# Down projections of 16 of 22 FFN tiles by seven block products instead of eight, and retention's prompt matmuls in another order

## The chip, the cores and the metric

The kernel runs on one core of a Trainium2 chip. The metric is the device time of one execution in microseconds. Before the change it is 1979.84 us, the median of three runs (1979.19 to 1980.41).

A core has a matrix engine (PE in the rows; its weight loads are listed apart as PEld), a vector engine (DVE), a scalar engine (ACT), GpSimd (POOL) and SyncE (SP), which issues most transfers. Each works through its own instructions in order. Matmuls write to PSUM, a small memory of banks that the vector and scalar engines read; everything else lies in SBUF.

## The reference, cut to what matters

One step of a two-layer decoder trunk on 512 prompt tokens and 8 sample tokens, in float32, width 1024. Each layer is

```
x += 0.5 * FFN1(rmsnorm(x))
z  = rmsnorm(x) @ w_in          # retention, windowed attention, conformer conv
x += concat(o_retention, o_attention, o_conv) @ w_out
x += 0.5 * FFN2(rmsnorm(x))
FFN(h) = (silu(h @ wg) * (h @ wu)) @ wd     # wg, wu: 1024 x 2816, wd: 2816 x 1024
```

Retention runs over chunks of 128 tokens with four heads: `o = (q k^T * decay) v + q S * decay`, where `S` is the state that the earlier chunks left.

## The kernel before, in words

Activations lie transposed: features on the 128 partitions, all 520 tokens along the row, so that x is 8 tiles of 128x520. A matmul covers one half of the tokens, 260. Full float32 accuracy comes from splitting each operand into a high part (rounded to the matrix engine's fast float32 format) and a low remainder, and adding three products: high weight with low data, high with high, low with high. This is `mm3` (L206 to L212): six matmuls of 128x260 for one 128x128 weight tile, three products on each half of the tokens.

Weights come in chunks of eight 128x128 tiles, 512 KB each, in the order of use. For each chunk SyncE loads it (`ensure_load`, L170), ACT rounds it to the high part (`split_hi`, L185, 128x1024) and DVE subtracts for the low part (`split_lo`, L192). Three chunks of each are buffered; `next_tile` starts the splits of the chunk two ahead whenever it enters a new one.

An FFN has 22 tiles of 128 hidden features, done in two groups of 11 (`NG`, `GF`). For each tile f the kernel computes gate and up (16 weight tiles, 96 matmuls), then DVE scales the gate (L288), ACT applies silu (L290), DVE scales the up part (L291) and multiplies (L292), and the product is split into high and low (L222 on ACT, L223 on DVE). When the 11 tiles of a group are there, the down projection loops over the 8 output tiles m; for each it adds 11 `mm3` products in PSUM, f from 0 to 10, and DVE adds half of the sum to x (L299). There are two layers with two FFNs each, so four FFNs.

PSUM is handed out in tiles of two banks, four of them in rotation (`ptile`). The program fixes the order on each engine by the order of the code (`manual_schedule`); between the FFNs the middle part (`mix`) follows a list of step names, `ORDER`. A wait on another engine is a semaphore and holds back everything behind it on the waiting engine.

In `mix`, `ret_prompt` computes retention for two chunks at a time (steps `ri2` and `ri0`). Its second half (L792 to L807) goes through the chunks and heads; for each it issues one matmul over all 128 partitions (L801, values times scores) and, for every chunk but the first, one over 64 partitions (L806, state times q; head 0 of a pair uses partitions 0 to 63, head 1 those from 64). These are plain float32 matmuls, and each leaves two records in the trace.

Of the kernel before, what the change touches and what calls it, by code (L numbers as in the profile page):

```python
# [10 lines left out]
F32 = mybir.dt.float32  # L11
# [11 lines left out]
NG = 2  # L23
GF = NF // NG
# [3 lines left out]
CT = 8  # L28
LNEXP, SILU = "natural_log_exp_and_others", "silu_and_others"
# [83 lines left out]

@with_exitstack
def step_kernel(ctx: ExitStack, tc: tile.TileContext, io: dict):
# [6 lines left out]
    wraw = pool("wraw", 3)  # L122
# [11 lines left out]
    R = const.tile([128, NT], F32, name="R")  # L134
    Rd = const.tile([128, 2, NT], F32, name="Rd")
# [33 lines left out]
    raw, spl, at, nxt, pending = {}, {}, [0], [0], []  # L169

    def ensure_load(i):
        if i < NCH and i not in raw:
            t = wraw.tile([128, CT * 128], F32, tag="w", name="w")
            nc.sync.dma_start(t, io["w"][i])
            raw[i] = t

    def split_hi(i):

        if i == nxt[0] and i < NCH:
            nxt[0] += 1  # L180
            ensure_load(i)
            t, raw[i] = raw[i], None
            h = wspl.tile([128, CT * 128], F32R, tag="wh", name="wh")
            lo = wspl.tile([128, CT * 128], F32R, tag="wl", name="wl")
            nc.scalar.copy(h, t)  # L185
            spl[i] = (h, lo)
            pending.append((i, t))

    def split_lo(n=9):
        for i, t in pending[:n]:  # L190
            h, lo = spl[i]
            nc.vector.tensor_sub(lo, t, h.bitcast(F32))  # L192
            ensure_load(i + 3)
        del pending[:n]

    def next_tile(ahead=True):
        i, c = divmod(at[0], CT)
        if c == 0 and ahead:
            for j in (i, i + 1, i + 2):
                split_hi(j)  # L200
            split_lo()
        at[0] += 1
        s = slice(c * 128, (c + 1) * 128)
        return spl[i][0][:, s], spl[i][1][:, s]
# [71 lines left out]

    def ffn(norm, after):
        for g in range(NG):
            hs = []
            for f in range(GF):  # L280
                first = g == 0 and f == 0
                og, ou = ptile(), ptile()
                for o, k in ffn_tiles(first, og, ou):
                    mm3(o, next_tile(), xh[:, k], xl[:, k], k == 0, k == KD - 1)
                if first:
                    run(norm)
                t, u = wt("t"), wt("u")
                nc.vector.tensor_mul(v2(t), og[:, :, :HN], v2(R))  # L288
                table(SILU)
                nc.scalar.activation(t, t, AF.Silu)  # L290
                nc.vector.tensor_mul(v2(u), ou[:, :, :HN], v2(R))  # L291
                nc.vector.tensor_mul(u, u, t)  # L292
                hs.append(v2(unit(F32R)))
                split(hs[f][:, 0], hs[f][:, 1], u)
            for m in range(KD):
                o = ptile()
                for f in range(GF):
                    mm3(o, next_tile(), hs[f][:, 0], hs[f][:, 1], f == 0, f == GF - 1)
# [3 lines left out]
                if g == NG - 1:  # L302
                    run(after(m))

    def mix(l, after):
# [467 lines left out]
        def ret_prompt(c0):  # L773
# [20 lines left out]
            oo = o.rearrange("p e (i a t) -> p e i a t", i=2, a=2)  # L794
            for i in range(2):
                c = c0 + i
                t = slice(c * 128, (c + 1) * 128)
                for h in range(4):
                    a, e = divmod(h, 2)
                    d, s = oo[:, e, i, a], slice(64 * e, 64 * e + 64)  # L800
# [84 lines left out]
        def chunk_hi():  # L885
            while True:
                split_hi(nxt[0])
# [31 lines left out]
    raw[0], raw[1] = (wraw.tile([128, CT * 128], F32, tag="w", name="w") for _ in range(2))  # L919
    spl[0], spl[1] = (  # L920
        tuple(wspl.tile([128, CT * 128], F32R, tag=t, name=t) for t in ("wh", "wl")) for _ in range(2)
    )
    nxt[0] = 2

# [22 lines left out]
    ensure_load(2)  # L947
    nc.sync.dma_start(cc, io["cc"])
    ensure_load(3)
    onef = const.tile([128, 128], F32, name="onef")  # L950
# [14 lines left out]
    for step in START:  # L965
        if step[0] == "h":
            half(half_split, int(step[1]))
        elif step[0] == "c":
            split_hi(int(step[1]))
# [23 lines left out]
def host_arrays(i):  # L993
# [16 lines left out]
    gu = [t.reshape(DEPTH, NG, -1, 128, 1024) for t in gu]  # L1010
    dn = [
        f[f"ffn{j}_wd"].reshape(DEPTH, NG, GF, 128, KD, 128).transpose(0, 1, 4, 2, 3, 5)
        .reshape(DEPTH, NG, GF * KD // CT, CT, 128, 128).transpose(0, 1, 2, 4, 3, 5)
        .reshape(DEPTH, NG, -1, 128, 1024)
        for j in (1, 2)
    ]
    ffn = [np.concatenate([g, d], axis=2).reshape(DEPTH, -1, 128, 1024) for g, d in zip(gu, dn)]
# [83 lines left out]
```

## Time and profile before

| | |
|---|---|
| median of three runs | 1979.84 us |
| the profiled execution, whole time | 1980.78 us |
| its span from first to last instruction | 1979.0 us |
| PE busy | 1955.9 us (99%), 16190 records |
| DVE busy | 984.2 us (50%) |
| ACT busy | 666.2 us (34%) |
| mean granted TensorE clock | 0.996 of full speed |

The profiled execution is 0.94 us above the median. Matmuls overlap in the engine's pipeline: one of 128x260 lasts 283 ns in its record, and the next starts 120 ns after it. What counts for the time is the distance from start to start; what counts for an engine that waits for a result is the end.

### The profile page before, as it was taken

To read this page: it belongs to the slowest core of one execution; us is meant where nothing else is said; L and a number is where in the kernel's file an instruction comes from. 1 tells how busy PE (TensorE), PEld (TensorE's weight loads), DVE (VectorE), ACT (ScalarE), POOL (GpSimd) and SP (SyncE) were. 2 spreads that over 40 slices of the span, in tenths; PEclk is the share of its full clock that TensorE was granted. 3 is DMA by queue.
4 is the path that set the end of the run, shared out by engine and by line. 5 is a ranking of instruction groups with operands and counts; after the bars stand their busy time and mean duration, and the time that the engine had idled before them with its cause. 6 is when DMAs were issued, how large, how long until landed. Compare 5 with 4: busy or idle time off the path is not lost.

```text
span 1979.0 us, 36417 instructions
## 1 busy us (share of the span) xinstructions
PE 1955.9 (99%) x16190; PEld 1936.6 (98%) x16190; DVE 984.2 (50%) x1311; ACT 666.2 (34%) x960; POOL 21.4 (1%) x48
## 2 busy tenths in 40 slices
PE   8999999999989999999999999999998999999999
PEld 8999999999889999999999999999997999999999
DVE  6443444488566443344444434445886564423442
ACT  5221223333665222222332212224337542212221
POOL 0000000000000000000000000000000000000000
PEclk9999999999999999999999999999999999999999
DMA  5222222333302222222222222223232122222231
GB/s 186 96 96 87 95 86 97 112 104 111 112 33 90 95 93 96 86 89 95 95 92 91 96 86 89 96 94 123 97 119 90 44 97 92 94 94 96 86 103 69
DMA packets 53581, 188.26 MB, mean 95 GB/s; under 512 B 6208, under 2 KB 6960, under 8 KB 53296
## 3 DMA queue, kind: packets, MB, share of 16 engines
q1 hardware_dynamic: 50784, 178.40, 26.6%
q0 software_dynamic: 2496, 7.43, 1.2%
q8 instruction: 127, 2.08, 0.4%
q14 instruction: 30, 0.25, 0.0%
q10 hardware_dynamic: 144, 0.11, 0.0%
HBM read 178.45 MB, written 7.45 MB: 94 GB/s over the span
## 4 chain that ended last, share of the span: by engine, by line
PE 97%; DVE 1%; ACT 1%; DMA 0%; issue 0%; SPq 0%; DVEq 0%
PE o L209 93%; PE o L228 1%; PE o L801 1%; PE o L806 0%; PE o L823 0%; DMA x<-in_x 0%; PE o L333 0%; PE o L594 0%; PE o L582 0%; DVE nt L246 0%; PE o L782 0%; DVE rr L247 0%; ACT rsq L836 0%; ACT m L567 0%; DVE m L859 0%
## 5 line engine op out<-in xcount | busy, mean ns | idle before, releaser
L209 PE MATMUL o<-xl,wh 128*128 128x260 f32 x3584 | 724.6, 283 | 7.2 <-DVE xl L254 5.9
L209 PE MATMUL o<-xh,wl 128*128 128x260 f32 x3584 | 723.0, 283 | 0.0
L209 PE MATMUL o<-xh,wh 128*128 128x260 f32 x3584 | 722.3, 283 | 0.0
L192 DVE TENSOR_TENSOR wl<-w,wh 128x1024 fp32r<-128x1024 f32 x318 | 389.0, 1224 | 424.7 <-ACT wh L185 422.7
L209 PEld LDWEIGHTS o<-xl,wh 128*128 128x128 f32 x3584 | 554.0, 189 | 8.4 <-ACT wh L222 5.8
L209 PEld LDWEIGHTS o<-xh,wl 128*128 128x128 f32 x3584 | 553.6, 189 | 0.0
L209 PEld LDWEIGHTS o<-xh,wh 128*128 128x128 f32 x3584 | 552.4, 189 | 0.0
L185 ACT CAST wh<-w 128x1024 fp32r<-128x1024 f32 x318 | 333.3, 1049 | 615.3 <-PE o L209 331.7
L209 PE MATMUL o<-m,wh 128*128 128x260 f32 x3072 | 493.0, 282 | 0.0
L209 PEld LDWEIGHTS o<-m,wh 128*128 128x128 f32 x3072 | 421.0, 188 | 0.0
L209 PE MATMUL o<-m,wl 128*128 128x260 f32 x1536 | 308.6, 282 | 0.0
L209 PEld LDWEIGHTS o<-m,wl 128*128 128x128 f32 x1536 | 236.5, 188 | 0.0
L291 DVE TENSOR_TENSOR u<-o,R 128x520 f32<-128x520 f32 x88 | 61.6, 699 | 248.6 <-PE o L209 248.6
L222 ACT CAST m<-u 128x520 fp32r<-128x520 f32 x88 | 55.2, 627 | 324.6 <-DVE u L292 324.6
L290 ACT ACTIVATE t<-t 128x520 f32<-128x520 f32 x88 | 56.2, 638 | 164.4 <-DVE t L288 164.4
L299 DVE SCALAR_TENSOR_TENSOR x<-o,x 128x520 f32<-128x520 f32 x64 | 44.7, 698 | 97.9 <-PE o L209 97.6
L223 DVE TENSOR_TENSOR m<-u,m 128x520 fp32r<-128x520 f32 x88 | 61.7, 701 | 61.1 <-ACT m L222 61.1
L411 DVE SCALAR_TENSOR_TENSOR m<-m,par 128x512 f32<-128x512 f32 x120 | 90.0, 750 | 2.9
L252 ACT ACTIVATE xh<-x,par 128x520 fp32r<-128x520 f32 x48 | 34.9, 729 | 99.3 <-DVE x L299 80.2
L292 DVE TENSOR_TENSOR u<-u,t 128x520 f32<-128x520 f32 x88 | 61.7, 701 | 9.2
L288 DVE TENSOR_TENSOR t<-o,R 128x520 f32<-128x520 f32 x88 | 60.9, 693 | 0.1
L254 DVE SCALAR_TENSOR_TENSOR xl<-x,par,xh 128x520 fp32r<-128x520 f32 x48 | 36.3, 758 | 21.5 <-ACT xh L252 21.5
(166 smaller groups left out, 664.8 us busy)
## 6 DMA issues: line engine op xcount, KB each, us to landing
w<-in_w SPq DMA_DIRECT2D x318, 512.0 KB, 3.2
out_y<-x SPq DMA_DIRECT2D x8, 260.0 KB, 2.3
m<-in_s_ret SPq DMA_DIRECT2D x4, 512.0 KB, 5.5
m<-sc POOLq DMA_DIRECT2D x8, 256.0 KB, 4.4
out_o_rets<-m POOLq DMA_DIRECT2D x4, 512.0 KB, 3.2
x<-in_x SPq DMA_DIRECT2D x3, 520.0 KB, 7.8
cc<-in_cc SPq DMA_DIRECT2D x1, 1092.0 KB, 10.4
w<-in_w SPq DMA_DIRECT2D x4, 256.0 KB, 6.4
```

Source lines behind the costliest of these rows:

```text
L185: nc.scalar.copy(h, t)
L192: nc.vector.tensor_sub(lo, t, h.bitcast(F32))
L209: nc.tensor.matmul(o[:, s, :HN], lhsT=a, rhs=b[:, s * HN : (s + 1) * HN], start=first and i == 0, stop=last and i == 2,)
L222: nc.scalar.copy(h, src)
L223: nc.vector.tensor_sub(lo, src, h.bitcast(F32))
L254: nc.vector.scalar_tensor_tensor(xl[:, k], x[:, k], g, xh[:, k].bitcast(F32), op0=ALU.mult, op1=ALU.subtract)
L288: nc.vector.tensor_mul(v2(t), og[:, :, :HN], v2(R))
L290: nc.scalar.activation(t, t, AF.Silu)
L291: nc.vector.tensor_mul(v2(u), ou[:, :, :HN], v2(R))
L292: nc.vector.tensor_mul(u, u, t)
L299: nc.vector.scalar_tensor_tensor(v2(x[:, m]), o[:, :, :HN], 0.5, v2(x[:, m]), op0=ALU.mult, op1=ALU.add)
L411: nc.vector.scalar_tensor_tensor(y[:, :SEQ], ub[:, j : j + SEQ], w, y[:, :SEQ], op0=ALU.mult, op1=ALU.add)
```

## The change

The 22 tiles form three groups, 8, 8 and 6. The first two are "paired": the down projection of such a group is seen as products of 2x2 blocks. The blocks of the weights are (even or odd f) by (even or odd m); the blocks of the data are (even or odd f) by (first or second half of the tokens). Eight block products make such a 2x2 product in the usual way; seven do in Winograd's scheme, with sums of blocks as operands. One block product is 12 matmuls of 128x260: four pairs of f (`JP`), three high/low products each. The third group stays as it was.

For one pair of output tiles m, m+1 the scheme needs the weight blocks a11, a12, a22 as they are and four sums s1 to s4, which DVE forms (`sums`, at most 128x512 each), and each of the seven is split into high and low by itself (128x512 on ACT and on DVE). On the data side `pair_blocks` forms four sums of 128x260 for each pair of tiles f and splits all seven blocks. `pair_down` runs the seven products and, between them, copies partial results from one PSUM place to another on ACT (three copies of 128x260) and adds to x on DVE (three of 128x520). It uses three PSUM tiles: `one` holds c11 and c21, `mid` holds m5, `two_` holds c12 and c22.

Raw weight chunks have four buffers rather than three. In `ret_prompt` all matmuls over 128 partitions of two chunks now come first, and then those over 64. The host lays the weights of the paired groups out in the new order.

```diff
-NG = 2
-GF = NF // NG
+GROUPS = ((0, 8, True), (8, 16, True), (16, 22, False))
+JP = 4
+PC = JP * 128
+PRODUCTS = ("a11", "s1", "s2", "a12", "s3", "s4", "a22")
+RAW = 4
+    def sums(u):
...
+        name, i = seq[u]
...
+        if name == "s1":
+            nc.vector.tensor_add(Rd[:, 0, :PC], a21, a22)
+        elif name == "s2":
+            nc.vector.tensor_sub(a21, a21, a11)
+            nc.vector.tensor_add(Rd[:, 1, :PC], a21, a22)
+        elif name == "s4":
+            nc.vector.tensor_sub(Rd[:, 0, :PC], a12, Rd[:, 1, :PC])
+    def split_hi():
+        u = nxt[0]
...
+            load()
+            sums(u)
+            spl[u] = parts_of(u)
+            nc.scalar.copy(spl[u][0], source(u))
+            pending.append(u)
+    def ahead(u):
+        old = len(pending)
+        while nxt[0] < len(seq) and slot[nxt[0] + 1] - slot[u] <= 6:
+            split_hi()
+        if seq[u][0] == "chunk":
+            split_lo()
+        else:
+            split_lo(old)
+            sums(nxt[0])
+    def product(name, o, blocks, first):
...
+        ahead(u)
...
+        for j in range(JP):
+            s = slice(j * 128, (j + 1) * 128)
+            bh, bl = blocks[j][name]
+            for i, (a, b) in enumerate(((h, bl), (h, bh), (lo, bh))):
+                nc.tensor.matmul(
+                    o, lhsT=a[:, s], rhs=b, start=first and j == 0 and i == 0, stop=j == JP - 1 and i == 2,
+                    skip_group_check=True,
+                )
+    def pair_blocks(u, w):
+        (b11, b12), (b21, b22) = ((z[:, :HN], z[:, HN:]) for z in (u, w))
+        p, q = wt("tp"), wt("tq")
+        nc.vector.tensor_sub(p[:, :HN], b12, b11)
+        nc.vector.tensor_sub(q[:, :HN], b12, b22)
+        nc.vector.tensor_sub(p[:, HN:], b11, q[:, :HN])
+        nc.vector.tensor_sub(q[:, HN:], b21, p[:, HN:])
...
+            (bh, bl, 0, HN, b11), (bh, bl, HN, NT, w), (th, tl, 0, NT, p), (th, tl, NT, NT, q),
+        ):
+            split(h[:, c : c + n], lo[:, c : c + n], src[:, :n])
...
+    def pair_down(m, blocks):
+        one, mid, two_ = ptile(), ptile(), ptile()
+        c11, c21, m5, c12, c22 = (t[:, i, :HN] for t, i in ((one, 0), (one, 1), (mid, 0), (two_, 0), (two_, 1)))
+        def add(half, src):
+            d = x[:, m : m + 2, half * HN : (half + 1) * HN]
+            nc.vector.scalar_tensor_tensor(d, src, 0.5, d, op0=ALU.mult, op1=ALU.add)
+        product("a11", c11, blocks, True)
+        nc.scalar.copy(c22, c11)
+        product("s1", m5, blocks, True)
+        add(1, m5.unsqueeze(1).to_broadcast([128, 2, HN]))
+        product("s2", c22, blocks, False)
+        nc.scalar.copy(c12, c22)
+        product("a12", c11, blocks, False)
+        product("s3", c22, blocks, False)
+        nc.scalar.copy(c21, c22)
+        product("s4", c12, blocks, False)
+        add(1, two_[:, :, :HN])
+        product("a22", c21, blocks, False)
+        add(0, one[:, :, :HN])
     def ffn(norm, after):
...
+            for f in range(a, b):
+                u = hidden(norm, f == 0)
+                if not paired:
+                    hs.append(v2(unit(F32R)))
+                    split(hs[-1][:, 0], hs[-1][:, 1], u)
+                elif f % 2:
+                    hs.append(pair_blocks(even, u))
+                else:
+                    even = u
+            if paired:
+                for m in range(0, KD, 2):
+                    pair_down(m, hs)
+                continue
...
-            for i in range(2):
-                c = c0 + i
-                t = slice(c * 128, (c + 1) * 128)
-                for h in range(4):
...
-                    nc.tensor.matmul(
-                        d, lhsT=ret["vtk"][c // 2][:, c % 2, h],
-                        rhs=au[:, i, e, a], start=True, stop=c == 0,
-                    )
-                    if c:
-                        nc.tensor.matmul(
-                            d, lhsT=ret["S"][s, c - 1, a], rhs=ret["q"][s, a, t], start=False, stop=True
-                        )
+            for i in range(2):
+                c = c0 + i
+                for a in range(2):
+                    for e in range(2):
+                        nc.tensor.matmul(
+                            oo[:, e, i, a], lhsT=ret["vtk"][c // 2][:, c % 2, 2 * a + e], rhs=au[:, i, e, a],
+                            start=i == 0 and a == 0, stop=c == 0, skip_group_check=True,
+                        )
+            for i in range(2):
...
+                        if c:
+                            nc.tensor.matmul(
+                                oo[:, e, i, a], lhsT=ret["S"][s, c - 1, a], rhs=ret["q"][s, a, t],
+                                start=False, stop=True, skip_group_check=True,
+                            )
```

Three places show how the order on an engine moves.

First DVE at the end of a group, from the last hidden tile on. Before, after the two multiplications (L291, L292) comes one subtraction (L223) for the tile's low part, then a chunk of weights (L192) and the first addition to x (L299):

```order
L291 TENSOR_TENSOR u<-o,R 128x520 [waits PE_49]
L292 TENSOR_TENSOR u<-u,t 128x520 [waits DVE_49,Activation_49]
L223 TENSOR_TENSOR m<-u,m 128x520 [waits Activation_49]
L192 TENSOR_TENSOR wl<-w,wh 128x1024 [waits DMAHW1_49,Activation_49]
L192 TENSOR_TENSOR wl<-w,wh 128x1024 [waits DMAHW2_49,PE_49,Activation_49]
L299 SCALAR_TENSOR_TENSOR x<-o,x 128x520 [waits PE_49]
```

Now four block sums (L401 to L404, tp and tq are p and q) stand ahead of the four low parts (L327), and the sum s4 of the weights (L235) behind them:

```order
L392 TENSOR_TENSOR u<-o,R 128x520 [waits PE_49]
L393 TENSOR_TENSOR u<-u,t 128x520 [waits DVE_49,Activation_49]
L401 TENSOR_TENSOR tp<-u 128x260
L402 TENSOR_TENSOR tq<-u 128x260 [waits DVE_49]
L403 TENSOR_TENSOR tp<-u,tq 128x260 [waits DVE_49]
L404 TENSOR_TENSOR tq<-u,tp 128x260 [waits DVE_49]
L327 TENSOR_TENSOR m<-u,m 128x260 [waits Activation_49]
L327 TENSOR_TENSOR m<-u,m 128x520 [waits Activation_49]
L327 TENSOR_TENSOR m<-tp,m 128x520 [waits Activation_49]
L327 TENSOR_TENSOR m<-tq,m 128x520 [waits Activation_49]
L235 TENSOR_TENSOR Rd<-w,Rd 128x512
```

So the low part of b11, the first thing of the last pair that the down projection reads, is the seventh instruction from L392 on, where the low part of the last tile was the third; and s4 comes behind all of them.

Second PE at the first set of seven products of a group (o is the PSUM tile; wh and wl are now just two buffers in turn). Before there is one stretch of matmuls with no wait on ACT inside an output tile but for new weights. Now the rows from s2's first matmul to s4's last are these:

```order
L305 MATMUL o<-m,wh 128x260 [waits Activation_49]
L305 MATMUL o<-m,wh 128x260 x11
L305 MATMUL o<-m,wl 128x260 x12
L305 MATMUL o<-m,wh 128x260 [waits Activation_49]
L305 MATMUL o<-m,wh 128x260
L305 MATMUL o<-m,wh 128x260 [waits DVE_49]
L305 MATMUL o<-m,wh 128x260 x9
L305 MATMUL o<-m,wl 128x260 [waits Activation_49]
L305 MATMUL o<-m,wl 128x260
L305 MATMUL o<-m,wl 128x260 [waits DVE_49]
L305 MATMUL o<-m,wl 128x260 x9
```

They are s2, a12 (the row of twelve), s3 and s4. On ACT, where before only the casts of whole chunks (L185) stood in a down projection, these are now its instructions from the cast of s3's and s4's weights on, with the three copies between the casts for the products ahead:

```order
L262 CAST wh<-w 128x512 [waits PE_49,Activation_49]
L262 CAST wl<-Rd 128x512 [waits DVE_49,PE_49]
L426 COPY o<-o 128x260 [waits PE_49]
L262 CAST wh<-w 128x512 [waits Activation_49]
L262 CAST wl<-w 128x512 [waits DMAHW3_49,PE_49,Activation_49]
L430 COPY o<-o 128x260 [waits PE_49]
L262 CAST wh<-Rd 128x512 [waits DVE_49,Activation_49]
L262 CAST wl<-Rd 128x512 [waits DVE_49,PE_49,Activation_49]
L433 COPY o<-o 128x260 [waits PE_49,Activation_49]
```

In the built program the three waits on ACT in the PE rows are, in turn, on the copies L426 (c22 from c11), L430 (c12 from c22) and L433 (c21 from c22): s4 writes c12, which shares the PSUM tile `two_` with c22, from which L433 reads.

Third PE in `ret_prompt`. Before, in step `ri2`:

```order
L801 MATMUL o<-m 128x128 [waits DVE_49]
L806 MATMUL o<-m 128x128 [waits DVE_49]
L801 MATMUL o<-m 128x128
L806 MATMUL o<-m 128x128
L801 MATMUL o<-m 128x128
L806 MATMUL o<-m 128x128 [waits DVE_49]
```

Now (L961 is the old L801, L972 the old L806):

```order
L961 MATMUL o<-m 128x128 [waits DVE_49]
L961 MATMUL o<-m 128x128 x7
L972 MATMUL o<-m 128x128 [waits DVE_49]
L972 MATMUL o<-m 128x128
L972 MATMUL o<-m 128x128 [waits DVE_49]
```

The two kinds took turns matmul by matmul; now eight of one are followed by eight of the other.

## Rows read from the trace of the kernel before

**Rows 1.** The page: busy time by engine, and the chain's shares by engine.

```profile
PE 1955.9 (99%) x16190; PEld 1936.6 (98%) x16190; DVE 984.2 (50%) x1311; ACT 666.2 (34%) x960; POOL 21.4 (1%) x48
PE 97%; DVE 1%; ACT 1%; DMA 0%; issue 0%; SPq 0%; DVEq 0%
```

**Rows 2.** PE's waits: us in total, times, longest us.

```profile
PE o L582 <- ACT m L576: 9.3, 2, 4.6
```

**Rows 3.** The chain in order of time: start us, us, what; first FFN.

```profile
21.58 374.51 PE o L209 x3120
```

**Rows 4.** Timeline of PE (start us, us) where a down projection begins.

```profile
136.50 0.40 PE L209 MATMUL o<-xh,wl 128*128 128x260 f32 x2
136.75 0.64 PE L209 MATMUL o<-m,wh 128*128 128x260 f32 x4
```

**Rows 5.** Timeline of DVE at the same place.

```profile
136.95 0.70 DVE L291 TENSOR_TENSOR u<-o,R 128x520 f32<-128x520 f32 x1 [3.05 <-PE o L209]
137.75 0.70 DVE L292 TENSOR_TENSOR u<-u,t 128x520 f32<-128x520 f32 x1
139.14 0.70 DVE L223 TENSOR_TENSOR m<-u,m 128x520 fp32r<-128x520 f32 x1 [0.69 <-ACT m L222]
```

**Rows 6.** Timeline of ACT at the same place.

```profile
138.49 0.63 ACT L222 CAST m<-u 128x520 fp32r<-128x520 f32 x1 [3.91 <-DVE u L292]
```

**Rows 7.** Groups by form: xcount | busy us, mean ns of one | idle before.

```profile
L417 DVE TENSOR_TENSOR cs<-m,par 128x248 f32<-128x248 f32 x4 | 1.6, 410 | 0.0
L223 DVE TENSOR_TENSOR wl<-w,wh 128x512 fp32r<-128x512 f32 x4 | 2.7, 687 | 0.5 <-ACT wh L222 0.5
L299 DVE SCALAR_TENSOR_TENSOR x<-o,x 128x520 f32<-128x520 f32 x64 | 44.7, 698 | 97.9 <-PE o L209 97.6
L602 ACT CAST m<-o 128x256 fp32r<-128x256 f32 x8 | 2.9, 368 | 7.4 <-PE o L594 7.4
L222 ACT CAST wh<-w 128x512 fp32r<-128x512 f32 x4 | 2.4, 607 | 0.6 <-DMA w<-in_w 0.6
```

**Rows 8.** Timeline of DVE: three subtractions with nothing to wait for.

```profile
560.02 1.91 DVE L864 TENSOR_TENSOR xl<-m,xh 128x520 fp32r<-128x520 f32 x3
```

**Rows 9.** Timeline of ACT: two casts with nothing to wait for.

```profile
557.93 1.15 ACT L862 CAST xh<-m 128x520 fp32r<-128x520 f32 x2
```

**Rows 10.** Timeline of PE after waits, around the first layer's retention output.

```profile
553.80 3.40 PE L622 MATMUL o<-m 128*32 128x128 f32 x16
559.96 0.51 PE L209 MATMUL o<-xl,wh 128*128 128x260 f32 x2 [0.61 <-DVE st L540]
```

**Rows 11.** The chain: retention scores, then `ri2` and `ri0`, first layer.

```profile
480.00 1.09 PE o L782 x16
...
529.18 0.22 PE o L801 x2
529.40 0.41 PE o L806 x2
...
535.24 0.42 PE o L806 x2
535.65 1.31 PE o L801 x10
...
539.92 1.07 ACT m L812 x2
...
559.96 2.04 PE o L209 x14
```

**Rows 12.** Stretches: length, busy of PE, PEld, DVE, ACT, POOL, then PEclk.

```profile
550.00:550.50 0.50, 0.00 (x0) 0.00 (x0) 0.50 (x1) 0.47 (x2) 0.00 (x0) 0.52 0.00 0
556.50:557.00 0.50, 0.50 (x5) 0.36 (x3) 0.47 (x2) 0.50 (x5) 0.00 (x0) 0.65 0.00 0
1533.00:1533.50 0.50, 0.50 (x4) 0.29 (x2) 0.50 (x1) 0.50 (x3) 0.00 (x0) 0.56 0.00 0
1536.50:1537.00 0.50, 0.50 (x7) 0.50 (x6) 0.47 (x2) 0.50 (x4) 0.00 (x0) 1.00 0.00 0
```

More of the change, by code (lines that the diff above doesn't have):

```diff
@@ L189, in split_lo @@
-    def split_lo(n=9):
[L190 to L193, printed above, removed]
-        del pending[:n]
[L196 to L200, printed above, removed]
-            split_lo()
-        at[0] += 1
-        s = slice(c * 128, (c + 1) * 128)
-        return spl[i][0][:, s], spl[i][1][:, s]
+    seq, slot = [], [0]
@@ new lines, in add_chunks, with add_products @@
+    def add_chunks(n):
+        for _ in range(n):
+            seq.append(("chunk", chunk[0]))
+            slot.append(slot[-1] + 2)
+            chunk[0] += 1
+    def add_products(n):
+        for _ in range(n):
+            for name in PRODUCTS:
+                seq.append((name, chunk[0]))
+                slot.append(slot[-1] + 1)
+            chunk[0] += 2
+    chunk = [0]
+    for _ in range(DEPTH):
+        for part in range(3):
+            if part == 1:
+                add_chunks(MIX_CHUNKS)
+                continue
+            for a, b, paired in GROUPS:
+                add_chunks(2 * (b - a) * KD // CT)
+                if paired:
+                    add_products(KD // 2)
+                else:
+                    add_chunks((b - a) * KD // CT)
@@ new lines, in step_kernel, with load @@
+    assert chunk[0] == NCH
+    raw, done, spl, ready = {}, set(), {}, set()
+    at, nxt, loaded, pending = [0, 0], [0], [0], []
+    def load(dma=True):
+        while loaded[0] < NCH and (loaded[0] < RAW or loaded[0] - RAW in done):
+            i = loaded[0]
+            loaded[0] += 1
+            raw[i] = wraw.tile([128, CT * 128], F32, tag="w", name="w")
+            if dma:
+                nc.sync.dma_start(raw[i], io["w"][i])
+    def sums(u):
+        if u >= len(seq) or u in ready:
+            return
+        ready.add(u)
+        name, i = seq[u]
+        if name == "chunk":
+            return
+        load()
+        (a21, a11), (a22, a12) = ((raw[j][:, :PC], raw[j][:, PC:]) for j in (i, i + 1))
+        if name == "s1":
[5 more added lines that the diff above has]
+            nc.vector.tensor_sub(Rd[:, 0, :PC], a12, Rd[:, 1, :PC])
@@ new lines, in source, with parts_of @@
+    def source(u):
+        name, i = seq[u]
+        if name == "chunk":
+            return raw[i]
+        if name[0] == "a":
+            return dict(a11=raw[i][:, PC:], a12=raw[i + 1][:, PC:], a22=raw[i + 1][:, :PC])[name]
+        return raw[i][:, :PC] if name == "s3" else Rd[:, int(name == "s2"), :PC]
+    def parts_of(u):
+        tag = ("wh", "wl")
+        if seq[u][0] == "chunk":
+            return tuple(wspl.tile([128, CT * 128], F32R, tag=t, name=t) for t in tag)
+        t = tag[slot[u] % 2]
+        w = wspl.tile([128, CT * 128], F32R, tag=t, name=t)
+        return w[:, :PC], w[:, PC:]
@@ L275, in norm, with hidden @@
         yield
-    def ffn(norm, after):
[L278 to L294, printed above, removed]
+    def hidden(norm, first):
+        og, ou = ptile(), ptile()
+        for o, k in ffn_tiles(first, og, ou):
+            mm3(o, next_tile(), xh[:, k], xl[:, k], k == 0, k == KD - 1)
+        if first:
+            run(norm)
+        t, u = wt("t"), wt("u")
+        nc.vector.tensor_mul(v2(t), og[:, :, :HN], v2(R))
+        table(SILU)
+        nc.scalar.activation(t, t, AF.Silu)
+        nc.vector.tensor_mul(v2(u), ou[:, :, :HN], v2(R))
+        nc.vector.tensor_mul(u, u, t)
+        return u
@@ L301, in ffn @@
                 )
-                if g == NG - 1:
+                if last:
                     run(after(m))
@@ L918, in step_kernel @@
     nc.scalar.dma_start(par, io["par"])
[L919 to L922, printed above, removed]
+    load(False)
+    spl[0], spl[1] = parts_of(0), parts_of(1)
     nxt[0] = 2
+    done.update((0, 1))
     def load_x(a, b):
```

90 lines of the change are left out of this document (57 added, 33 removed).

## The prediction

> **What bounds the kernel now.** Read the page's busy shares and its chain first: PE is busy for 1955.9 of 1979.0 us and the chain is 97% PE [rows 1]. So only two things can change the time: the distance from one matmul to the next, and new idle time on PE. The list of waits comes next. PE's largest is 9.3 us in two waits of about 4.6 us, in the middle part of each layer [rows 2]; the FFNs, which are most of the span, have none worth a row. The chain in order of time gives the price of an FFN matmul: 3120 in 374.51 us, 120.0 ns each [rows 3]. DVE is busy half of the time and ACT a third, and both have been hidden. The question is what the change asks of them, and when.
>
> **What is removed: matmuls.** A pair of output tiles of a paired group took 2 x 8 `mm3` of six matmuls, 96; now 7 x 12 = 84. There are 4 such pairs in a group, 2 groups in an FFN and 4 FFNs: 32 sets of products, 384 matmuls fewer. At 120.0 ns that is **-46.1 us**. Each matmul keeps its form (128x260, a weight load of its own), so I leave its price alone; twelve in a row now add into one place, which is a rival below.
>
> **What is moved: retention.** In the chain every L801 and L806 between 529.18 and 535.65 takes 0.42 us for two records, and so do those of `ri0` that alternate. The row of ten L801 (1.31 us) is one such 0.42 and four matmuls at 0.22 [rows 11]. Matmuls over 64 partitions that alternate between the halves, as L806's will, are L782: 16 records in 1.09 us, 0.136 per matmul. A round of one L801 and one L806 thus costs 0.83 where the two alone would cost 0.36, and the turn and return cost 0.48. `ri2` (8 + 8 matmuls) falls from 6.47 to 8 x 0.22 + 8 x 0.136 + 0.48 = 3.33 us, `ri0` (8 + 4) from 4.24 to 2.79: 4.6 us a layer. The chain leaves PE at the end of `ri0` (539.92) and goes through ACT and DVE to the first output projection at 559.96; nothing else feeds it, so the start moves and all of it follows. Both layers: **-9.2 us**; between -7 (a quarter lost to other work on ACT) and -10.7 (no cost for the turns).
>
> **What is added, 1: the gap at the end of each paired group.** Let the first product matmul start where the first down matmul starts now, 136.75 [rows 4]. The last pair of tiles is read from the tenth matmul on, 136.75 + 9 x 0.12 = 137.83. Its first operand is the low part of b11. DVE scales at 136.95 and multiplies at 137.75 to 138.45 [rows 5]. Four sums and the low part follow. An op of 128x248 takes 0.41 us [rows 7], so 0.42 for 260; with nothing to wait for, the next one starts about 0.09 before the end of the last (three of 0.69 in 1.91) [rows 8]. So p starts at 138.36, q at 138.69; the second halves need q and then p, 139.13 and 139.57; the low part 139.90 to 140.32. The handoff to PE costs some 0.05, as from PE to DVE (136.62 + 0.28 against 136.95) [rows 4, 5]. PE goes on at 140.37, 2.54 late. A matmul that waited also does not have its weights loaded: the pair at 559.96 takes 0.51 us where a pair takes 0.40 [rows 4, 10], 0.10 more. Gap: 2.64 us. Eight groups: **+21.1 us**, between 8 x 2.2 (sums fully overlapped) and 8 x 3.1 (no overlap on DVE).
>
> **2: a second gap just behind it.** a11 and s1 then run until 140.47 + 15 x 0.12 = 142.27, and s2 needs the copy L426. On ACT it stands behind the cast of s4's weights, which needs the sum s4 on DVE, which stands behind the other three low parts: these start at 140.23, 140.84 and 141.45, the sum at 142.06 to 142.75 (0.69 for 128x512 [rows 7]). The cast takes 0.61, and the next ACT instruction starts 0.09 before its end, as two casts of 0.62 do in 1.15 [rows 9]: copy from 143.29. A copy from PSUM to PSUM stands nowhere in the trace; the nearest row is L602, 0.37 from PSUM to SBUF [rows 7]. PE goes on at 143.71, 1.44 late, with the weights 1.54. Eight times: **+12.3 us**, between 8 x 0.9 and 8 x 2.2 (a copy of 0.15 or 0.60, and the five instructions ahead of it twice as close or not overlapped).
>
> **3: a wait in every set.** s4 waits for the copy L433, and that copy needs s3, the product just before. From the slot after s3's last matmul: 0.16 until that matmul ends (0.28 long, 0.12 apart), 0.04 to ACT [rows 5, 6], 0.37 copy, 0.05 back, 0.10 for the weights: 0.72. In three sets of four ACT is also held by the cast of the next s2. Its sum is the sixth DVE instruction from the addition that waits for s1: 0.21 after s1's last slot, four at 0.61, then 0.71 until the difference it needs is there, 0.69 for the sum, 0.54 until ACT is past the cast, 4.59 us; s3 ends and reaches ACT at 3 x 1.44 + 0.20 = 4.52. So 0.07 more there, 0.75 x 32 = **+24.0 us**, between 32 x 0.5 (a copy of 0.15) and 32 x 1.1 (the DVE instructions in that row at their full 0.69 and 0.70 [rows 7]).
>
> **Costed at nothing.** The other copies: c22 in later sets and c12 have a whole product, 1.44 us, between their source and their user. DVE in a set: eleven ops of 128x512 and three of 128x520, 0.61 apart, 8.5 us beside 10.1 of PE; the cover is thin, and is a rival. The third group: its last tile's low part ends at 139.84 [rows 5], and is read after 5 x 6 matmuls, 140.35. The loads: as many bytes, with one buffer more.
>
> **Sum.** -46.1 - 9.2 + 21.1 + 12.3 + 24.0 = +2.1 us on the profiled execution's 1980.78: 1982.9. That execution lies 0.94 above the median of the runs, so I forecast **1982 us**, practically no change: the saving is eaten by waits of its own.
>
> **Rivals.**
>
> *The wait in every set costs nothing.* s4 neither reads nor writes what L433 touches: c12 is one bank of `two_`, c22 the other. For it: the copy's result is first used by a22, a product later. Against it: the wait stands in PE's order, and a semaphore holds PE whatever the memory could do; where PE waited for ACT in this trace, it stood still [rows 2]. Price: 1982 - 24 = **1958 us**. The Trainium skill (PSUM — Partial Sum Buffer, "PSUM bank collisions raise a hardware error") says that two engines on different banks run clean, so the chip itself would need no wait there; by that rule the time would be this rival's. No row here shows a copy beside matmuls into the same tile's other bank.
>
> *The clock falls at each group's end.* During both idles of 4.6 us the granted clock fell to half, and it came back 6.8 us later in the first layer (550.0 to 556.7) and 3.5 in the second (1533.0 to 1536.5) [rows 2, 12]. The two gaps here are 2.6 and 1.5 us with 1.8 us of matmuls between. For it: the sum is 4.2. Against it: matmuls between. At half clock L622's record takes 0.21 us, twice the 0.11 of L801 [rows 10, 11], so a matmul of 0.12 takes some 0.10 more. For 3.5 us most of the loss falls into the second gap; for 6.8 us some 16 matmuls more are slow, 1.6 us a group. That is +12.8 us: **1995 us**, slower than before. From two of the eight groups on it takes the time past no change.
>
> *DVE becomes the bound in the sets.* It has 8.5 of 10.8 us at the close spacing; at full durations 9.7. With its waits for s1, s4 and a22 it has no free order. If it loses 0.4 us a set: +12.8, **1995 us**. For it: the six DVE instructions from the addition after s1 to the next s2's sum already reach L433. Against it: its low parts are ready five products ahead.
>
> *Matmuls into one place are slower.* At 10 ns more, 2688 matmuls make +27 us, **2009 us**. Against it: L622 adds eight matmuls into one place, in the 0.21 us a record just named, the price of any other at half clock [rows 10].
>
> *Retention doesn't do what it says.* If the alternation is not what costs there, -9.2 goes: **1991 us**.
>
> **How the numbers follow.** The forecast 0.56, with its terms between 1973 and 1991; no wait in the sets 0.13; the clock 0.13; DVE 0.10; slower matmuls 0.02; retention 0.06. What a measurement can tell from no change is about 0.2%, 4 us: 1975.9 to 1983.8. The forecast's own range gives 0.14 faster, 0.28 same, 0.14 slower; the first rival is faster; the others give 0.25 slower and 0.06 same, where only part of them comes. Faster 0.27, same 0.34, slower 0.39. All low ends of the terms together give 1964, all high ends 2004. The range 1963 to 1997 leaves out some 0.10 of the no-wait case and 0.08 at the slow end of the others.
>
> **What would show it.** In the changed kernel's waits of PE: L305 on DVE's low part (L327) eight times, about 2.5 us; L305 on ACT's copy L426 eight times, about 1.4; L305 on L433 32 times, about 0.65. PE should have 16190 - 384 records and lie idle some 55 us more. L961 and L972 should take about 3.3 and 2.8 us, and the output projection follow 20 us after them as before. I am wrong if L433 is not in that list, if the granted clock falls behind a group, if L305's distance is not 120 ns, or if PE waits in a set for an addition to x (L423) or for low parts of weights (L268).

## The result, and the profile after

The changed kernel takes 1989.33 us (median of four runs, 1987.89 to 1989.87), the kernel before, on the same chip, 1979.51 (1978.13 to 1980.41). The ratio is 1.005, 95% interval 1.0034 to 1.0066: 9.8 us slower. The range of the prediction holds it; the forecast of 1982 us was 7 us too low.

The page's busy times and chain shares, as in [rows 1]:

```profile
PE 1921.3 (97%) x15806; PEld 1897.0 (96%) x15806; DVE 1234.5 (62%) x1855; ACT 791.0 (40%) x1280; POOL 21.4 (1%) x48
PE 87%; DVE 8%; ACT 3%; issue 1%; DMA 0%; SPq 0%; ACTq 0%; DVEq 0%
```

The 384 matmul records are gone. The chain has lost a tenth of PE to DVE and ACT. PE's waits, as in [rows 2]:

```profile
PE o L305 <- DVE m L327: 19.8, 8, 2.5
PE o L305 <- ACT o L433: 18.1, 32, 0.6
PE o L742 <- ACT m L736: 9.2, 2, 4.6
PE o L305 <- ACT o L426: 4.8, 6, 1.3
```

Of the three forecast waits, two stand there as forecast; the third, L426, is shorter than forecast and absent in two groups. PE lies idle 41 us longer in all than before (64.5 us against 23.1), where the prediction had some 55. PE's timeline in the first paired group, where it takes the place of [rows 4], shows why:

```profile
105.15 0.62 PE L305 MATMUL o<-m,wh 128*128 128x260 f32 x3 [2.47 <-DVE m L327]
105.61 2.74 PE L305 MATMUL o<-m,wl 128*128 128x260 f32 x12
108.56 1.93 PE L305 MATMUL o<-m,wh 128*128 128x260 f32 x12 [0.22 <-ACT o L426]
110.33 1.61 PE L305 MATMUL o<-m,wl 128*128 128x260 f32 x12
113.88 1.71 PE L305 MATMUL o<-m,wl 128*128 128x260 f32 x12 [0.51 <-ACT o L433]
```

These are a11's last three, s1, s2, a12 and (after s3) s4. s1 takes 2.74 us, where a12, as long a product, takes 1.61. The stretches (columns as in [rows 12]: PEclk is the third number from the end) behind gap 1 of the first, the third and the fourth paired group:

```profile
105.60:108.40 2.80, 2.75 (x14) 2.44 (x12) 2.66 (x6) 1.18 (x3) 0.00 (x0) 0.51 0.00 0
706.60:713.00 6.40, 5.46 (x26) 5.16 (x25) 6.23 (x11) 2.85 (x6) 0.00 (x0) 0.50 0.49 158
843.00:850.00 7.00, 4.02 (x32) 3.60 (x30) 5.92 (x12) 2.42 (x5) 0.00 (x0) 1.00 0.01 2
```

After PE stood still for 2.5 us the granted clock fell from 1.00 to 0.50 in six groups, for some 3.4 us in four and 7 in two, and did not in two. Yet s2 starts 7.12 us after its group's first product in all eight: behind a fast s1 it waits 1.35 us for the copy, behind a slow one 0 to 0.9. The copy itself, on ACT, stands behind the cast of s4's weights, as the prediction had it:

```profile
107.62 0.62 ACT L262 CAST wl<-Rd 128x512 fp32r<-128x512 f32 x1 [1.62 <-DVE Rd L235]
108.14 0.37 ACT L426 COPY o<-o 128x260 f32<-128x260 f32 x1
```

Even s4's start in the first set is reached by a chain without PE in it (the chain in order of time: start us, us, what):

```profile
104.75 2.17 DVE m L327 x4
106.92 0.61 DVE Rd L235
...
107.62 0.63 ACT wl L262
...
112.01 0.70 DVE Rd L233
...
112.81 0.63 ACT wl L262
...
113.46 0.37 ACT o L433
...
113.88 6.06 PE o L305 x48
```

From the late tile's low parts DVE runs with hardly a free moment to the sum that ACT's cast ahead of the copy L433 needs. So a slow matmul before 113.88 costs nothing unless it is slow for long.

All eight paired down projections, from the first product to the next gate matmul, last 48.2, 48.0, 50.2, 48.0, 48.2, 48.1, 50.0 and 48.0 us (388.7 together; the two of 50 are those with 7 us of half clock). Without waits they would take 8 x 336 x 0.120 = 322.6. So 66 us of waits and slow matmuls stand against 46.1 saved: +20 us in the FFNs.

Retention gives 10 us of it back. Its stretch in the first layer, as in [rows 11]:

```profile
529.30 1.95 PE L961 MATMUL o<-m 128*128 128x128 f32 x16
531.18 1.16 PE L972 MATMUL o<-m 64*128 64x128 f32 x16
532.27 2.05 PE L961 MATMUL o<-m 128*128 128x128 f32 x16
534.25 0.71 PE L972 MATMUL o<-m 64*128 64x128 f32 x8
534.80 1.13 PE L715 MATMUL o<-m 64*128 64x256 f32 x8
```

5.5 us, where the kernel before took 10.7; the first output projection then starts at 555.21, 20.4 us behind it, nearly as before (20.0 from `ri0`'s copies on [rows 11]). But the chain no longer passes these matmuls. It comes over DVE and ACT to the copies of their result, which now run one after the other:

```profile
534.10 0.20 ACT m L667
534.30 1.94 ACT m L979 x4
```

So ACT sets the path here now, and making these matmuls shorter still would gain next to nothing.

### The profile page after: what moved, and what is told of

Read it like the earlier page. It is cut to its first block, busy times and chain, and to the rows that moved or that the text cites. A ratio compares the mean times of both kernels' runs of the same rounds, so it can differ in the third digit from the quotient of the medians.

```text
span 1985.8 us, 36650 instructions
## 1 busy us (share of the span) xinstructions
PE 1921.3 (97%) x15806; PEld 1897.0 (96%) x15806; DVE 1234.5 (62%) x1855; ACT 791.0 (40%) x1280; POOL 21.4 (1%) x48
## 4 chain that ended last, share of the span: by engine, by line
PE 87%; DVE 8%; ACT 3%; issue 1%; DMA 0%; SPq 0%; ACTq 0%; DVEq 0%
PE o L313 74%; PE o L305 11%; DVE wl L268 1%; DVE m L327 1%; DVE Rd L233 1%; DVE wh L268 1%; DVE w L232 1%; DVE Rd L230 1%; PE o L332 1%; ACT o L433 1%; ACT wl L262 1%; PE o L990 0%; PE o L493 0%; DMA x<-in_x 0%; DVE nt L350 0%
## 5 line engine op out<-in xcount | busy, mean ns | idle before, releaser
L262 ACT CAST wh<-w 128x1024 fp32r<-128x1024 f32 (+1 forms) x318 | 305.8, 963 | 436.9 <-PE o L313 300.8
L268 DVE TENSOR_TENSOR wl<-w,wh 128x1024 fp32r<-128x1024 f32 x254 | 310.0, 1222 | 213.8 <-ACT wh L262 212.5
L392 DVE TENSOR_TENSOR u<-o,R 128x520 f32<-128x520 f32 x88 | 61.5, 699 | 256.5 <-PE o L313 256.5
L305 PE MATMUL o<-m,wh 128*128 128x260 f32 x1344 | 187.9, 289 | 33.4 <-DVE m L327 19.8
L305 PEld LDWEIGHTS o<-m,wh 128*128 128x128 f32 x1344 | 172.5, 192 | 40.2 <-DVE m L327 21.4
L305 PE MATMUL o<-m,wl 128*128 128x260 f32 x1344 | 188.5, 291 | 9.2 <-ACT o L433 9.2
L305 PEld LDWEIGHTS o<-m,wl 128*128 128x128 f32 x1344 | 176.1, 196 | 12.6 <-ACT o L433 12.6
L313 PE MATMUL o<-m,wh 128*128 128x260 f32 x1024 | 164.4, 282 | 0.0
L313 PEld LDWEIGHTS o<-m,wh 128*128 128x128 f32 x1024 | 140.3, 188 | 0.0
L326 ACT CAST m<-u 128x260 fp32r<-128x260 f32 (+1 forms) x88 | 47.7, 542 | 210.9 <-DVE u L393 210.9
L423 DVE SCALAR_TENSOR_TENSOR x<-o,x 128x520 f32<-128x520 f32 x96 | 66.9, 697 | 69.6 <-PE o L305 69.6
L313 PE MATMUL o<-m,wl 128*128 128x260 f32 x512 | 102.8, 282 | 0.0
L313 PEld LDWEIGHTS o<-m,wl 128*128 128x128 f32 x512 | 78.9, 188 | 0.0
```

Of the source, the lines that this page charges most:

```text
L262: nc.scalar.copy(spl[u][0], source(u))
L268: nc.vector.tensor_sub(lo, source(u), h.bitcast(F32))
L305: nc.tensor.matmul(o, lhsT=a[:, s], rhs=b, start=first and j == 0 and i == 0, stop=j == JP - 1 and i == 2, skip_group_check=True,)
L313: nc.tensor.matmul(o[:, s, :HN], lhsT=a, rhs=b[:, s * HN : (s + 1) * HN], start=first and i == 0, stop=last and i == 2,)
L326: nc.scalar.copy(h, src)
L423: nc.vector.scalar_tensor_tensor(d, src, 0.5, d, op0=ALU.mult, op1=ALU.add)
```

## The experiments

**Retention alone.** The kernel before, with this in `ret_prompt` in place of the one loop over chunks and heads:

```diff
             for i in range(2):
...
+                            oo[:, e, i, a], lhsT=ret["vtk"][c // 2][:, c % 2, 2 * a + e], rhs=au[:, i, e, a],
...
+            for i in range(2):
...
+                                oo[:, e, i, a], lhsT=ret["S"][s, c - 1, a], rhs=ret["q"][s, a, t],
```

> The kernel before with only the retention part of the change. Theory (each change between matmuls over 128 and over 64 partitions costs time, and the sorting saves it on the path): the stretch from the first of these matmuls to the sample scores shrinks by 5.1 us a layer (before 529.02 to 540.75 us, changed kernel 529.30 to 535.95 us), nothing behind it gives it back, so 10 us less: 1969 to 1970 us; if the half clock that the kernel before shows at 506 to 512 us is away too, as it is in the changed kernel, another 3 us less: 1966. Rival (the matmuls shrink, but ScalarE's and VectorE's steps behind them set the end): 1976 us or more.

Measured: 1969.35 us, ratio to before 0.9944 (0.9932 to 0.9956), 10.5 us faster. The theory holds, and the order pays in full: nothing behind it takes the gain back, beyond some 0.2 us a layer. The profiled execution took 1966.89 us, what was expected where the half clock at 506 to 512 us is away. With the result this leaves +20 us for the products, the sum just read from the groups. The kernel before has a stretch at half clock in the first layer's middle part:

```profile
506.00:512.00 6.00, 6.00 (x21) 5.23 (x22) 1.23 (x3) 4.99 (x9) 0.00 (x0) 0.50 0.48 159
```

The same stretch of this kernel is at full clock, as it is in the changed kernel:

```profile
506.00:512.00 6.00, 6.00 (x45) 5.77 (x45) 2.26 (x4) 5.37 (x9) 0.00 (x0) 1.00 0.35 124
```

PE's instructions up to there are the same in this kernel and the one before, so the order of retention's matmuls, which come later, does not decide this fall; it is worth some 3 us of the first layer when two single traces are compared.

**c12 out of c22's tile, into the free half of `mid`.**

```diff
-        c11, c21, m5, c12, c22 = (t[:, i, :HN] for t, i in ((one, 0), (one, 1), (mid, 0), (two_, 0), (two_, 1)))
+        c11, c21, m5, c12, c22 = (t[:, i, :HN] for t, i in ((one, 0), (one, 1), (mid, 0), (mid, 1), (two_, 1)))
-        add(1, two_[:, :, :HN])
+        for i, c in ((0, c12), (1, c22)):
+            d = x[:, m + i, HN:]
+            nc.vector.scalar_tensor_tensor(d, c, 0.5, d, op0=ALU.mult, op1=ALU.add)
```

> The changed kernel, with c12 moved from the PSUM tile two_ into the free half of mid, and the last 520-wide addition to x made as two of 260. Theory (s4 waits for the copy L433 only because c12 and c22 lie in one tile): the 32 waits of 0.62 us go, with the drain and the weight load before them 0.87 us each, 27.8 us in all: 1961 to 1963 us. Rival 1 (the wait stands for an order that the data need): same time, 1989 us, the wait stays. Rival 2 (VectorE, busy 8.8 us of a set's 11.0 us, 9.0 of 10.1 then, becomes the bound): the wait turns up elsewhere in the sets, and 1975 us or more remain.

Measured: 1960.69 us, ratio 0.9904 (0.9891 to 0.9917); 28.6 us less than the changed kernel. PE's waits in the sets are then:

```profile
PE o L305 <- DVE m L327: 19.7, 8, 2.5
PE o L305 <- ACT o L426: 2.6, 3, 1.4
```

No wait for L433 is left and none has come in its place (the copy still runs, in the first set from 113.02 us on, now beside s4, which starts at 112.82): the wait came from the shared tile alone, and DVE is not the bound in a set (rivals 1 and 2 fall). Where c12 lies made the difference between slower and faster than before.

**The even tile's blocks early.** `pair_blocks` begins when the even tile is there and ends with the odd one:

```diff
         nc.vector.tensor_sub(p[:, :HN], b12, b11)
+        split(bh[:, :HN], bl[:, :HN], b11)
+        split(th[:, :HN], tl[:, :HN], p[:, :HN])
+        w = yield
...
-                    hs.append(pair_blocks(even, u))
+                    hs.append(even.send(u))
```

> The changed kernel, with the blocks that need only the even tile of a pair (b11 and b12-b11, for a11 and s1) formed and split before the odd tile is ready. Theory (gap 1 and gap 2 end on one chain: a11 and s1 now run at once, but s2 waits for the copy L426, which ScalarE does behind four casts and the sum of s4, at about 108.0 us in place of 108.4): s2 starts 0.5 us earlier in the first group, 1984 to 1986 us in all, and PE then shows one wait for L426 of 3 to 4 us in each of the 8 groups. Rival (gap 1 is a cost by itself): 2.6 us less in each group, 1968 us.

Measured: 2001.14 us, ratio 1.0098 (1.0078 to 1.0119): slower than the changed kernel, which neither theory said. The waits are those of the theory:

```profile
PE o L305 <- ACT o L427: 31.0, 8, 3.9
PE o L305 <- ACT o L434: 17.7, 32, 0.6
```

L427 is the copy L426 and L434 the copy L433. a11 and s1 run at once, and s2 starts at 6.90 us in place of 7.12. But now the clock falls in all eight groups, during s2's wait, and s2 and a12 behind it are slow. PE's timeline of this kernel in the first group:

```profile
108.04 2.97 PE L305 MATMUL o<-m,wh 128*128 128x260 f32 x12 [3.86 <-ACT o L427]
110.81 2.80 PE L305 MATMUL o<-m,wl 128*128 128x260 f32 x12
```

Their 2.8 to 3.0 us, where 1.6 is the rule, are matmuls at half clock, as the stretches show:

```profile
108.00:110.00 2.00, 1.96 (x9) 1.96 (x10) 2.00 (x4) 1.05 (x2) 0.00 (x0) 0.50 0.69 217
110.00:113.00 3.00, 3.00 (x16) 3.00 (x16) 2.75 (x5) 0.89 (x2) 0.00 (x0) 0.50 0.61 199
```

In the changed kernel the slow matmuls were followed by a wait that hid them; here they are followed by matmuls. The groups take 400.8 us, 12.1 more than in the changed kernel, which is the whole difference of 11.8. So work moved into the gap, with the gap's end nearly where it was, was worth nothing, and the place of the gap decides what the clock costs.

**The sum of s4 early.**

```diff
         if seq[u][0] == "chunk":
             split_lo()
+            if u + 1 < len(seq) and seq[u + 1][0] == "a11":
+                sums(nxt[0])
+                sums(nxt[0] + 1)
```

> The changed kernel, with the sum for s4 in a group's first set (L235) put on VectorE before the last tile's work, so that ScalarE's cast of it doesn't hold the copy L426. Theory (the clock, at its lower level after gap 1 in 6 of 8 groups, makes a11's last and s1's matmuls slow, and these cover gap 2): the wait for L426 goes, but where the clock falls this gives 0.2 to 0.4 us a group, and about 1.5 in the two others, together 4 to 5 us: 1984 to 1985.5 us. Rival (gap 2 costs 1.54 us in all 8 groups, as the prediction had it): 1977 us.

Measured: 1983.01 us, ratio 1.0018 (1.001 to 1.0027), 6.3 us less than the changed kernel: near the theory, not at the rival. No wait for L426 is left. What holds the rest is s4. In PE's timeline the first row is from a group with half clock and the second from one without (L436 is the copy L433):

```profile
113.91 1.71 PE L308 MATMUL o<-m,wl 128*128 128x260 f32 x12 [0.51 <-ACT o L436]
715.88 1.71 PE L308 MATMUL o<-m,wl 128*128 128x260 f32 x12 [1.39 <-ACT o L436]
```

These starts lie 12.1 and 11.5 us behind the first product. At full clock the time won before s4 mostly becomes a longer wait of s4, at the end of DVE's chain. Such a group takes 47.2 us, one with half clock 47.8 to 48.0.

**The gap filled with matmuls.** The kernel just shown, and in gap 1 of each group:

```diff
+            if fill is not None and j == JP - 1:
+                for _ in range(20):
+                    nc.tensor.matmul(fill, lhsT=h[:, :128], rhs=blocks[0][name][0], start=True, stop=True)
```

> The changed kernel with the sum for s4 early, and 20 more matmuls of 128x260 (2.4 us) in gap 1 of each group, into a place that nothing reads; the gap itself, and what ends it, stay. Theory (the clock falls because PE stands still in gap 1, and the 27 matmuls behind it then take 1.6 us more, in 6 of 8 groups): the granted clock stays at 1.00 in all 8, and the time is 9 to 10 us under that of the kernel without these matmuls, 1983 us: 1973 to 1974 us. Rival (the fall has another cause, such as the change from 520 to 260 columns): half clock stays, 1983 us or a little more.

Measured: 1981.13 us, ratio 1.0005 (0.9996 to 1.0014), 1.9 us less. The clock stays up in all eight groups; the stretch is that of s1 and s2 in the first:

```profile
105.00:109.00 4.00, 3.91 (x33) 3.89 (x33) 4.00 (x8) 3.23 (x7) 0.00 (x0) 1.00 0.12 18
```

So the fall comes from PE standing still: the rival falls. My 9 to 10 us were wrong: I counted the slow matmuls at their full price, though the run before had shown s4 waiting behind them. All groups now take 47.2 us, 0.63 less in the six that had fallen: 4 us by the trace, of which the medians show 2, hardly clear of noise (the two intervals overlap). Why the clock falls in six groups and not in two stays open.

**All three waits taken away.** c12 in `mid`, the even blocks and the sum early, and in a group's first set:

```diff
+                    if f == b - 1:
+                        first = pair_down(0, hs)
+                        next(first)
+                    hs[-1].update(even.send(u))
```

`next(first)` issues a11, the copy into c22 and s1; `even.send(u)` then forms the late tile's blocks.

> The changed kernel with c12 in mid (as in the run of that name), the even tile's blocks early, the sum for s4 early, and in a group's first set a11, the copy L426 and s1 issued before the odd tile's blocks, so that on ScalarE the copy stands ahead of these blocks' casts. Theory (all that the FFNs lose is these three waits and the lower clock behind them): no wait of PE in the sets over 0.5 us, the granted clock 1.00 through the group starts, and 39 us less than with c12 in mid alone (the FFNs' 67.0 us of waits and slow matmuls less the 27.7 of the L433 waits): 1921 to 1926 us. Rival 1 (VectorE, 9.0 us of work in a set of 10.1 us and the late tile's blocks on top, becomes the bound at the group starts): 1 to 2 us a group remain, 1930 to 1938 us. Rival 2 (the clock falls after the change from 520-column to 260-column groups, wait or not): rows of half clock at the group starts, 1935 us or more.

Measured: 1946.5 us, ratio 0.9829 (0.9814 to 0.9844): 32 us faster than before, but 20 more than the theory's upper end and more than rival 1 allowed. Rival 2's time fits, but not its sign: the clock stays up at the group starts. The waits left in the sets:

```profile
PE o L309 <- ACT o L441: 13.4, 8, 1.7
PE o L309 <- ACT o L444: 4.3, 8, 0.5
```

With the time until the matmul before them ends these are 8 x (1.84 + 0.69) = 20 us, what was missing. L441 is the copy into c12: it waits until DVE has added m5 to x, since c12 now shares `mid` with m5, and DVE is late with that behind the late tile's low parts. Moving c12 had bought a new shared tile; rival 1 names the right engine, but for the most part its order did this and not the amount of its work, as the next run shows.

**The order on DVE and ACT.** m5's addition ahead of the late tile's low parts, and each copy ahead of the cast that its product looks ahead to; of the edit, the lines for the copy behind s2:

```diff
-        product("s2", c22, blocks, False)
+        product("s2", c22, blocks, False, False)
         nc.scalar.copy(c12, c22)
+        look()
```

> The kernel of the last full version (c12 in mid, even blocks and sum early, first copy early) with the two waits that it still showed taken away by order alone: VectorE's addition of m5 to x ahead of the late tile's low parts (the copy into c12 waited for it, 1.67 us in each of 8 groups, since m5 and c12 share mid), and on ScalarE each copy issued ahead of the cast that the next product looks ahead to (0.5 us in each). Theory (these waits, 8 x (1.84 + 0.69) = 20 us with drain and weight loads, are all that is left): 1926 us, 1924 to 1930, with no wait of PE in the sets over 0.4 us. Rival (VectorE's backlog at the group start, 3.2 us of the late blocks on sets that leave it 1.1 us each, only moves the wait on to the casts' low parts): 1934 us or more, with waits for L268 in the first or second set.

Measured: 1933.9 us, ratio 0.9767 (0.9754 to 0.978), 46 us faster than before. The page's busy times:

```profile
PE 1906.9 (99%) x15806; PEld 1889.2 (98%) x15806; DVE 1253.3 (65%) x1919; ACT 791.8 (41%) x1312; POOL 21.4 (1%) x48
```

DVE has as many instructions as in the run before (x1919), and no more time. PE's only wait in the sets:

```profile
PE o L309 <- ACT o L452: 3.9, 8, 0.5
```

The groups take 331.4 us, 9 above the 322.6 without waits. L452 is the copy into c21; it still stands behind one cast that waits for a sum on DVE (L230), and with the end of the matmul before and the weight load behind that is 6 of the 8 us by which the run misses the theory's 1926; the theory wanted no wait over 0.4 us. So the time is the lower edge of the rival's, and the rival is right that a piece of DVE's backlog remains, though not where it looked (no wait for L268). Of the 20 us of the run before, order alone brought 12.6.

**Retention by twos, and by halves.** The matmuls over 128 and 64 partitions in turns of two (the two loops over `e` stand in one loop over `i` and `a`), and, in a second kernel, those over 64 with e outside:

```diff
-            for i in range(2):
+            for e, i in ((0, 0), (0, 1), (1, 0), (1, 1)):
```

> The changed kernel with the retention's matmuls in turns of two over 128 partitions and two over 64 (one per half e), so that a turn-over comes 11 times in the two calls of a layer, where the kernel before has 23 and the changed one 2, and no matmul follows the one before it into the same place. Theory (each turn-over costs 0.24 us: (10.6 - 5.5) / 21): the stretch from the first of these matmuls to the sample scores takes 7.5 to 7.9 us, 2.2 us a layer over the changed kernel. Rival (what cost was the second matmul waiting for the first one's place): 5.5 us, no change.

> The changed kernel with the matmuls over 64 partitions sorted once more, all of the lower half (e = 0) and then all of the upper half (e = 1). Theory (neighbours on different halves of the partitions run side by side, which is why 16 of them take 1.16 us where 16 over 128 partitions take 1.95): they take 1.95 us for 16, so the two calls 1.3 us a layer more. Rival (over 64 partitions each is shorter by itself): no change.

Each ran once, in 1991.95 and 1989.97 us against the changed kernel's 1989.33, so only their stretches are read here. The first takes 7.1 us from 530.61 to 537.67 where the changed kernel takes 5.5; rows of PE's timeline:

```profile
531.14 0.49 PE L969 MATMUL o<-m 64*128 64x128 f32 x4
531.56 0.71 PE L962 MATMUL o<-m 128*128 128x128 f32 x4
532.20 0.49 PE L969 MATMUL o<-m 64*128 64x128 f32 x4
```

So the turns cost, whatever place the matmul before wrote to: (7.06 - 5.50) / 8 = 0.20 us each. Before, with turns of one, it was (10.7 - 5.5) / 20 = 0.26, so a quarter is something else. The Trainium skill (TensorEngine Tiling (Array Packing), "Key Properties") says that changing the tiling mode drains the engine; turns that cost by themselves agree with it, and the 0.20 us is this run's.

The second kernel, PE's timeline:

```profile
533.97 1.71 PE L971 MATMUL o<-m 64*128 64x128 f32 x16
537.59 0.72 PE L971 MATMUL o<-m 64*128 64x128 f32 x8
```

Sixteen take 1.64 us from start to next start in place of 1.09, eight take 0.55 as before. Equal stretches show how many records run in each (x behind PE's busy time), first in the changed kernel, over 128 partitions and then over 64 with the halves in turn:

```profile
529.60:530.00 0.40, 0.40 (x6) 0.40 (x6) 0.40 (x3) 0.39 (x2) 0.00 (x0) 1.00 0.79 317
531.60:532.00 0.40, 0.40 (x12) 0.40 (x10) 0.23 (x1) 0.14 (x1) 0.01 (x1) 1.00 0.55 113
```

Then in the second kernel's sixteen, from their first start on:

```profile
533.96:534.50 0.54, 0.54 (x5) 0.53 (x5) 0.03 (x1) 0.54 (x1) 0.44 (x1) 1.00 0.53 106
534.50:535.04 0.54, 0.54 (x10) 0.54 (x9) 0.48 (x1) 0.03 (x1) 0.00 (x0) 1.00 0.22 30
535.04:535.58 0.54, 0.54 (x7) 0.44 (x4) 0.51 (x2) 0.00 (x0) 0.00 (x0) 1.00 0.84 144
```

So lower and upper half run side by side, two records in the 0.11 us of one. Of the lower half's eight in a row the first four run alone; the upper half's first starts 6 ns behind the lower's fifth (534.522 and 534.516 us), and only the middle is doubled. The row of eight has four of each half, and all of it is doubled. That fits both rows, so the theory holds in part: halves in turn are not needed, but a long row of one half runs alone. It also accounts for the quarter: before, each L806 stood between two matmuls over 128 partitions, without a neighbour on the other half. That is 0.11 us for each of 12, 1.3 us, and with 20 turns at 0.20 it makes the 5.2 us.

## Why the prediction came out as it did

*Products, -46.1.* Right: 384 records fewer at the same 0.120 us (a product's starts lie 1.44 apart). The rival of slower matmuls into one place falls.

*Retention, -9.2.* Right in mechanism, a little small: -10.5 alone. The two calls took 2.97 and 2.53 us where I had 3.33 and 2.79. They hold three turns of 0.20 us, 0.6 in all, where I had charged 0.96; and a matmul over 64 partitions took 0.11 us and not 0.136, since the row of L782 that I had read holds turns of its own. (The bound of -10.7 without any turns should have been -11.1 by the same rows.) That nothing else feeds the path was not so: ACT's copies now wait for ACT's own chain, though it cost only some 0.2 us a layer.

*Gap 1, +21.1.* Right: 2.47 us of idle, with drain and weight load 2.73 against 2.64, eight times 21.8.

*Gap 2, +12.3, and the clock.* Right in place: s2 starts at 7.12 us, 1.51 late and 1.60 with its weights where I had 1.54, with the clock up. The clock's fall, which I had as a rival and as a sign of being wrong, came in six groups beside it. In four it costs 0 to 0.2 us, because the slow matmuls end before the copy does; in the two where half clock lasted 7 us it costs 2.0 and 2.2. I had named both, "most of the loss falls into the second gap" and 1.6 us a group for 6.8 us. The error was to give them as one rival, all or nothing: the sum lacked 4.5 us. And the two gaps are no prices that a repair gets back one by one: with gap 1 alone taken away the time rose, with gap 2's wait alone it fell by 6.3 us, since s4 waits behind both.

*The wait in every set, +24.0.* Right in mechanism and 3 us small, of which 0.7 is a slip (0.72, and 0.07 more in three of four, is 0.77 a set, 24.7): 0.6 idle and 0.26 around it, 0.84 a set, 27 in all; taking it away gave 28.6. The copy from PSUM to PSUM takes 0.37 us, the row I had picked. The rival without this wait argued that s4 touches nothing that the copy does. That is so for the data, and the Trainium skill (PSUM — Partial Sum Buffer, "PSUM bank collisions raise a hardware error") lets two engines work in different banks at once. The run with c12 in `mid`, where s4 does not wait for the copy out of c22's bank, came to 1960.7 us, which agrees with the rule and with that rival's price of 1958; but the order in the program went by whole tiles of two banks, so the rule did not decide here.

*DVE as the bound in the sets.* No: without the shared tile the sets run at full rate. DVE's order decides at the group starts only, where it carries the late tile's blocks as well.

By the groups: 66.1 us of waits and slow matmuls against 57.4 forecast, 8.7 more, of which the clock has 4.5 and L433 2.9. Less retention's extra 1.3 us this is 7.4: the 7 us missed. But the trace is of the profiled executions, which lie 7.1 us apart where I had 2.1: 5.0 more. The other 2.4 are about the first layer's 3 us of half clock, which only the kernel before's execution has, so it is in part luck that the sum meets the medians this closely.

## What to carry to other kernels

A sum of waits is no sum when they end on one chain: find the instruction at which the chain rejoins PE (here those behind the copies L426 and L433), and count only what moves that. A dependency that goes by whole tiles can cost more than the arithmetic saved, so give a value that is copied out while its neighbour is written a tile of its own, and look at who shares the new tile. On an in-order engine, put the short instruction that PE waits for ahead of the long ones that look ahead.

## What the hardware showed that I had not expected

- An idle of 2.5 us on PE was followed by half clock in six groups of eight, and by none in two with the same instructions (with c12 in `mid` it was seven of eight, with the sum early six, and not the same six); 20 matmuls of no use in that idle kept the clock at 1.00 in all eight.
- A slow clock can be free: with PE's next wait set by another engine, s1 at 2.74 us in place of 1.61 left the group at 48.2 us, as against 48.0.
- A turn between matmuls over 128 and over 64 partitions costs 0.20 us; matmuls over the lower and the upper 64 partitions run side by side, 0.11 us for two records, where they stand near each other in the order.
